# Three small reductions of a hybrid decoder trunk, each computed another way

## The chip, the cores and the metric

The kernel runs on one core of a Trainium2 chip. The metric is the device time of one execution in microseconds. Three executions of the kernel before took 813.9, 815.08 and 815.81 us; the median is 815.08 us.

## The reference

Two decoder layers over 256 tokens of width 1024. A layer normalises the stream, makes one wide projection of it, and feeds three causal mixers side by side: a Mamba-2 state-space branch, sliding-window attention and "forgetting" attention. Each mixer's output is projected back, the three are merged under sigmoid gates, projected once more and added to the residual.

```python
def rms_norm(x, w):
    y = xf * lax.rsqrt(jnp.mean(xf * xf, axis=-1, keepdims=True) + NORM_EPS)
...
for layer in range(DEPTH):
    h = rms_norm(x, norm_w[layer])
    proj = jnp.einsum('bsd,de->bse', h, w_in[layer])          # 1024 -> 12832 columns
    ...
    y_a = mamba2_branch(...)        # dt = softplus(..), a_cum = cumsum(dt * a) in chunks of 128 tokens
    y_b = sliding_window_branch(...)
    y_c = forgetting_attention_branch(...)   # cum = cumsum(log_sigmoid(f)) over all 256 tokens
    branch = jnp.einsum('bsiw,iwd->bsid', ys, w_proj[layer])
    merged = jnp.sum(sigmoid(gates + gate_bias[layer]) * branch, axis=2)
    x = x + jnp.einsum('bsd,de->bse', merged, w_out[layer])
return rms_norm(x, final_norm_w)
```

Three places of it matter here:

- **Row roots.** `rms_norm` of the first layer multiplies each token's row by the reciprocal root of its mean square: 256 numbers.
- **Running sums.** For each layer two running sums over the tokens: 16 heads of the state-space branch (restarting at token 128) and 16 heads of the forgetting attention (running through all 256 tokens).
- **Group sums.** The state-space branch ends in a normalisation of its 1024 channels in 4 groups of 256. For every token and every group, the sum of squares is needed: 4 x 256 numbers a layer.

## The kernel before

Weights are float32 and come from DRAM in pieces of 512 KB through SyncE's queue (L363), into one of six buffers `raw`. ScalarE rounds each piece to a high part `hi` (L293) and VectorE takes the rest as `lo` (L294); both feed TensorE at its fast float32r rate. Activations are kept in the same two parts, and a dense product is three passes: hi x hi, lo x hi, hi x lo. A piece's buffer becomes free, and SyncE can issue a later load into it, when VectorE has made its `lo`.

Products without such parts, the small ones of this document among them, use plain float32, which TensorE does in two passes; each pass is one record of the profile.

The program is a list of operations (`op`, from L1249 on): for each layer the value projections, keys and queries of the window attention, the convolution channels of the state-space branch, then gates and output projections. Small work is launched as a generator (`launch`, L115) that does a part, yields a delay, and is taken up again by `pump` (L150) when the planner's own count of TensorE time, `clock["t"]`, has passed the delay. The delays are constants at the top (`D_CUM`, `D_GN1`, `D_GN2` and so on). So TensorE's order is written out by the planner. The order on the other engines and on SyncE's queue is made by the tile framework's scheduler, except in the first part of the program, whose order is written by hand (L1405 to L1531). `ends_later` holds small pieces of work that are issued after a later operation's eviction (`finish`, L846).

PSUM has two sets of banks: `pmm()` hands out three in turn for the dense products (L78), `pmx()` five for everything else. A bank can be written again only when what was in it has been read by ScalarE or VectorE.

The three places:

- **Row roots** (`normalize`, L1373, first layer only). The first projections are made from the unnormalised stream and scaled as they are read out (`y.rn`, two numbers in each partition: tokens 0 to 127 and 128 to 255). For the keys of the window attention the channels lie in the partitions, so the 256 roots must stand in every partition. ScalarE scales two copies of the identity with the roots (L1377), and TensorE multiplies them by a matrix of ones (L1381), which leaves the roots in a PSUM bank, the same in all partitions. VectorE multiplies the stream by it (L1387), and the result is split into `hi` and `lo` (L1388, by L293 and L294). The keys (`u_bk`, L567) are the first user; the queries (`u_bq`) follow. Each is two halves of 16 matmul records.
- **Running sums** (`decay_logits`, L765). VectorE computes the logits' softplus by a polynomial and leaves the rates in `rates`, as 128 tokens x (2 chunks, 2 kinds, 16 heads). TensorE then makes the running sums with a triangular matrix: L799 with the tokens in the partitions, L801 with the heads in the partitions, one product per chunk, each writing 32 partitions, and L803 adds the first chunk's totals to the second chunk of the forgetting heads. The sums go to DRAM (`cumd`, L810).
- **Group sums** (`group_norms`, L959). `squares` are four tiles, one per group, 128 channels x 256 tokens. With a half of such a tile as weights, a product with two columns of ones gives the sums with the tokens in the partitions: eight products of two columns (L966). VectorE scales them (L968), GpSimd takes the power -1/2 (L969), and VectorE makes a Newton step. The roots are first used in `u_proj_normed` (L980), which stands several operations later.

Of the kernel before, what the change touches and what calls it, by code (L numbers as in the profile page):

```python
# [11 lines left out]
F32 = mybir.dt.float32  # L12
F32R = mybir.dt.float32r
AF = mybir.ActivationFunctionType
ALU = mybir.AluOpType

P = 128
S = 256
# [4 lines left out]
EPS = 1e-6  # L23

D_SOFT, D_SOFT2, D_EVAC, D_SSD, D_SSD2 = 7.0, 3.0, 3.0, 8.0, 4.0
D_K, D_Q, D_QK, D_G0, D_FOX, D_BDMA, D_BIAS, D_BC, D_SSD3 = 6.0, 5.5, 2.0, 8.0, 0.0, 4.0, 2.6, 5.5, 1.0
D_GN1, D_GN2, D_CUM, D_H, D_M = 8.0, 13.5, 17.0, (4.8, 6.4), 5.0
BUDGET = 1.35
T_PP, T_SSD, T_BIAS = 1, 1, 1
D_MEET = 12.0  # L30
# [20 lines left out]
def hybrid_trunk(  # L51
# [5 lines left out]
    nc = tc.nc  # L57
# [5 lines left out]
    dr = ctx.enter_context(tc.tile_pool(name="dr", bufs=1, space=bass.MemoryType.DRAM))  # L63
# [17 lines left out]
    def pmx():  # L81
        return PS("mx", 5)

    act = nc.scalar.activation
    stt = nc.vector.scalar_tensor_tensor
    tt = nc.vector.tensor_tensor
    ts = nc.vector.tensor_scalar
# [15 lines left out]
    def mm(o, a, b, **kw):  # L103
        n = b.free_size()
        if a.dtype == F32R:
            clock["t"] += max(0.094, n / 2350.0)
        else:
            clock["t"] += max(0.2, n / 587.0) * (0.5 if a.free_size() == 64 or a.shape[0] == 32 else 1.0)
        nc.tensor.matmul(o, a, b, **kw)  # L109

    def transpose(o, a, i):
        clock["t"] += 0.109
        nc.tensor.transpose(o, a, i)  # L113
# [76 lines left out]
    ident = T("ident", [P, P])  # L190
    make_identity(nc, ident)
    tri = T("tri", [P, P])
# [11 lines left out]
    ones = onesr.bitcast(F32)  # L204
# [15 lines left out]
    def bc(ap, axis, n):  # L220
        s = list(ap.shape)
        s.insert(axis, n)
        return ap.unsqueeze(axis).to_broadcast(s)
# [66 lines left out]
    def split(hi, lo, src, scale=None, keep=lambda f: f):  # L290

        if scale is None:
            keep(act)(hi, src, AF.Copy)  # L293
            keep(tt)(lo, src, hi.bitcast(F32), op=ALU.subtract)  # L294
        else:
            keep(act)(hi, src, AF.Copy, scale=scale)
            keep(stt)(lo, src, scale, hi.bitcast(F32), op0=ALU.mult, op1=ALU.subtract)
# [130 lines left out]
    for l in range(L):  # L428
        y = Layer()
# [325 lines left out]
    def logits(y, t, i, p):  # L755

        if y.u is None:
            y.u = T("u", [P, 2, 32])
        o, b = y.u[:, t, 16 * i:16 * i + 16], y.hb[:, 16 * i:16 * i + 16]
        tt(o, p, b, op=ALU.add)  # L760
        y.logits += 1
        if y.logits == 4:
            launch(1, decay_logits(y), 0.0)

    def decay_logits(y):  # L765
        u = y.u
# [12 lines left out]
        s2f = s2.rearrange("p t c -> p (t c)")  # L779
        sf = s.rearrange("p t c -> p (t c)")  # L780
        ts(q, s2f, 1.0 / 19.0, None, op0=ALU.mult)
        for m in (17, 15, 13, 11, 9, 7, 5, 3):
            stt(q, q, 1.0 / m, s2f, op0=ALU.add, op1=ALU.mult)
        stt(q, q, 1.0, sf, op0=ALU.add, op1=ALU.mult)
        q3 = q.rearrange("p (t c) -> p t c", t=2)
        y.dt = T("dt", [P, 2, 16])
        rates = T("rates", [P, 2, 2, 16])
        lf = tmp[:, 2, :, 0:16]
        ts(w[:, :, 0:16], u[:, :, 0:16], 0.0, 0.5, op0=ALU.max, op1=ALU.mult)
        tt(y.dt, w[:, :, 0:16], q3[:, :, 0:16], op=ALU.add)  # L790
        ts(y.dt, y.dt, 2.0, None, op0=ALU.mult)
        ts(w[:, :, 16:32], u[:, :, 16:32], 0.0, 0.5, op0=ALU.min, op1=ALU.mult)
        tt(lf, w[:, :, 16:32], q3[:, :, 16:32], op=ALU.subtract)
        ts(rates[:, :, 0, :], lf, -16.0, None, op0=ALU.mult)
        tt(rates[:, :, 1, :], y.dt, bc(y.nega, 1, 2), op=ALU.mult)
        yield D_CUM

        pc = pmx()
        mm(pc[:, P:P + 32], tri, rates[:, :, 1, :], start=True, stop=True)  # L799
        for c in range(2):  # L800
            mm(pc[32 - 32 * c:64 - 32 * c, 0:P], rates[:, c, :, :].rearrange("p w c -> p (w c)"), tri,  # L801
               start=True, stop=(c == 0))
        mm(pc[0:16, 0:P], rates[:, 0, 0, :], ones, start=False, stop=True)  # L803
        y.acum = T("acum", [P, 2, 16])
        act(y.acum, pc[:, P:P + 32].rearrange("p (t c) -> p t c", t=2), AF.Copy)
        cum = T("L1", [64, P])
        act(cum, pc[0:64, 0:P], AF.Copy)
        y.cumd = dr.tile([2, 16, S], F32, name=f"cumd{y.l}", tag=f"cumd{y.l}")
        for c in range(2):
            nc.scalar.dma_start(y.cumd[:, :, c * P:(c + 1) * P].rearrange("w c s -> (w c) s"),  # L810
                                cum[32 - 32 * c:64 - 32 * c, :])


    def u_conv(y, u, c):
# [144 lines left out]
    def group_norms(y, squares):  # L959


        p = pmx()
        for g, q in enumerate(squares):
            for t in range(2):
                c = 4 * g + 2 * t
                mm(p[:, c:c + 2], q[:, t * P:(t + 1) * P], ones[:, 0:2], start=True, stop=True)  # L966
        v, r0 = T("sm", [P, 8]), T("sm", [P, 8])
        ts(v, p[:, 0:16].rearrange("p (g i) -> p g i", i=2)[:, :, 0], 1.0 / 256, 4 * EPS, op0=ALU.mult, op1=ALU.add)  # L968
        gtt(r0, v, mhalf, op=ALU.pow)  # L969

        def newton():
            y.roots = T("rs", [P, 8], bufs=4)
            tt(v, r0, v, op=ALU.mult)
            tt(v, v, r0, op=ALU.mult)
            stt(y.roots, v, -3.0, r0, op0=ALU.add, op1=ALU.mult)

        ends_later.append(newton)
        yield 0.0
# [274 lines left out]
    for y in layers:  # L1253
        l = y.l
        w = w_in[l]
# [8 lines left out]
        def cols(c0, n=256):  # L1264
            return sub([(0, w[:, c0:c0 + n])], n)
# [39 lines left out]
        if l == 0:  # L1305
            v, cv0, cv1 = cols(C_BV), cols(C_CV), cols(C_CV + 256)
            op(v, *(u_bv(y, t, first) for t in range(2)))
            op(None, lambda: layer_consts(y0, nc.gpsimd))
            op(None, lambda: launch(9, normalize(y0), 0.0))
            op(cv0, u_cv(y, 0, 0), u_cv(y, 0, 1))  # L1310
            op(cv1, u_cv(y, 256, 0), u_cv(y, 256, 1))
            gp.pop(0)()
            op(None, lambda: tables(fin["rope"]))
            op(None, lambda: normalized(y0))
        else:
            cv0, v = cols(C_CV, 512), cols(C_BV)
            op(None, lambda: drain(5))
            op(cv0, u_cv(y, 0, 0))
            op(v, u_bv(y, 0))
            op(None, lambda: drain(6))  # L1320
            op(cv0, u_cv(y, 0, 1))
            op(v, u_bv(y, 1))
            gp.pop(0)()
# [48 lines left out]

    def normalize(y):  # L1373

        rb = T("L1", [P, S])
        for t in range(2):
            act(rb[:, t * P:(t + 1) * P], ident, AF.Copy, scale=y.rn[:, t:t + 1])  # L1377
        yield 2.0
        p = pmx()
        for t in range(2):  # L1380
            mm(p[:, t * P:(t + 1) * P], ones, rb[:, t * P:(t + 1) * P], start=True, stop=True)  # L1381
        both_streams(y)
        hTh, hTl = y.normal
        for k in (0, 4):
            for t in range(2):
                xk = xw[:, t, k:k + 4, :]
                tt(xk, xk, bc(p[:, t * P:(t + 1) * P], 1, 4), op=ALU.mult)  # L1387
                split(hTh[:, t, k:k + 4, :], hTl[:, t, k:k + 4, :], xk)  # L1388
        yield 0.0

# [14 lines left out]
    with tc.manual_schedule(engines={ENG.PE, ENG.DVE, ENG.Activation, ENG.Pool}):  # L1405
# [11 lines left out]
        p = pmx()  # L1417
# [93 lines left out]
        for i in range(2):  # L1511
# [57 lines left out]
```

## Time and profile before

| what | value |
|---|---|
| median of three executions | 815.08 us |
| profiled execution, time | 813.07 us |
| its span | 811.4 us |
| TensorE busy | 800.2 us, 99% |
| VectorE busy | 683.8 us, 84% |
| ScalarE busy | 533.4 us, 66% |
| GpSimd busy | 172.7 us, 21% |
| moved by DMA | 170.43 MB, mean 210 GB/s |
| granted TensorE clock | 0.998 |

The span goes from the first instruction to the last; the time of the execution is a little longer. A row of the timeline has the start in us from the span's start, the length in us, the engine (PE is TensorE, DVE VectorE, ACT ScalarE, POOL GpSimd; SPq is SyncE issuing a DMA), the line, the operation, `out<-in`, shapes and a count; in brackets stands how long the engine was idle ahead of it and what ended that. For a matmul, `128*32 128x128` means 128 rows and 32 columns of weights, then the streamed tile. Neighbouring records of the same names are merged into one row, with the shape of the largest. Lines L109 and L113 are the helpers that issue all matmuls and transposes. A DMA row ends in the size of one transfer and the time from issue to landing.

### The profile page before, as it was taken

The page shows a single profiled execution, that of the slowest core. Times are in us where ns is not written, and L with a number is a line of the kernel's source. Part 1 is how long each engine was busy: PE and PEld are TensorE (multiplying, and loading weights), DVE is VectorE, ACT ScalarE, POOL GpSimd, SP SyncE. Part 2 cuts the span into 40 slices and gives each one's busy share as a digit, 9 for nine tenths or more (in the row PEclk, how much of TensorE's full clock was granted, in tenths as well). Part 3 has the DMA queues.
Part 4 walks back from the last instruction along what each step waited for, and adds up shares of the span by engine and source line. Part 5 has one row for each costly group of instructions (what it writes and reads, how often), then busy time and mean ns, then how long its engine had stood idle before and what let it go on. Part 6 is the DMA issues. An engine that isn't in the chain of part 4 may idle for free.

```text
span 811.4 us, 14867 instructions
## 1 busy us (share of the span) xinstructions
PE 800.2 (99%) x5178; PEld 714.2 (88%) x5178; DVE 683.8 (84%) x1412; ACT 533.4 (66%) x1142; POOL 172.7 (21%) x227
## 2 busy tenths in 40 slices
PE   8999999999999999999999999999999999999996
PEld 8998988888888888888998899888888988888896
DVE  6869999978998998776775799999879989869865
ACT  7777767865875785543565678677747677745452
POOL 3167113130321000130001741122313410002000
PEclk9999999999999999999999999999999999999999
DMA  9998888699675565667688987689986645566632
GB/s 311 279 262 183 240 221 203 197 261 252 175 211 163 164 191 180 211 208 246 214 261 259 241 209 220 159 214 257 272 253 175 212 130 160 172 228 218 210 106 77
DMA packets 139418, 170.43 MB, mean 210 GB/s; under 512 B 9976, under 2 KB 107072, under 8 KB 139344
## 3 DMA queue, kind: packets, MB, share of 16 engines
q1 hardware_dynamic: 114960, 140.53, 55.9%
q0 software_dynamic: 12928, 12.68, 9.8%
q10 hardware_dynamic: 11456, 16.28, 7.1%
q8 instruction: 41, 0.67, 0.3%
q14 instruction: 33, 0.27, 0.1%
HBM read 154.71 MB, written 2.16 MB: 193 GB/s over the span
## 4 chain that ended last, share of the span: by engine, by line
PE 96%; DMA 2%; DVE 1%; ACT 1%; issue 0%; SPq 0%; DVEq 0%
PE mm L109 83%; PE mx L109 10%; PE mx L113 3%; DMA raw<-in_w_in_dram 1%; DMA raw<-in_w_proj_dram 1%; DMA hb<-in_sinks_dram 0%; DVE lo L294 0%; ACT L L695 0%; ACT hi L293 0%; SPq L363 0%; SPq L189 0%; DVE L L1431 0%; DVE L L1127 0%; DVE L L1128 0%; ACT L L1435 0%
## 5 line engine op out<-in xcount | busy, mean ns | idle before, releaser
L109 PE MATMUL mm<-L,hi 128*128 128x512 f32 x1056 | 354.6, 387 | 0.3
L294 DVE TENSOR_TENSOR lo<-raw,hi 128x1024 fp32r<-128x1024 f32 (+1 forms) x276 | 313.1, 1153 | 37.8 <-ACT hi L293 36.6
L109 PE MATMUL mm<-hi,L 128*128 128x512 f32 (+2 forms) x1168 | 303.3, 349 | 0.1
L293 ACT ACTIVATE hi<-raw 128x1024 fp32r<-128x1024 f32 (+1 forms) x276 | 265.6, 981 | 51.1 <-PE mm L109 37.1
L109 PE MATMUL mm<-L,lo 128*128 128x256 f32 x1056 | 266.6, 273 | 0.0
L109 PEld LDWEIGHTS mm<-hi,L 128*128 128x128 f32 x1168 | 206.0, 190 | 22.6 <-issue 1.0
L109 PEld LDWEIGHTS mm<-L,hi 128*128 128x128 f32 x1056 | 195.2, 190 | 28.0 <-issue 5.2
L109 PEld LDWEIGHTS mm<-L,lo 128*128 128x128 f32 x1056 | 202.1, 191 | 5.3
L109 PE MATMUL mm<-lo,L 128*128 128x512 f32 (+2 forms) x584 | 201.5, 347 | 0.0
L109 PEld LDWEIGHTS mm<-lo,L 128*128 128x128 f32 x584 | 110.2, 190 | 10.7
L491 POOL DMA_DIRECT2D L<-L x68 | 60.1, 908 | 198.2 <-ACT L L490 153.8
L1057 POOL TENSOR_SCALAR_AFFINE_SELECT bias<-bias 128x128 f32<-128x128 f32 x64 | 40.7, 671 | 69.3 <-DMA bias<-cumd 69.2
L829 DVE SCALAR_TENSOR_TENSOR L<-L,vec,L 128x255 f32<-128x255 f32 (+2 forms) x96 | 46.2, 481 | 2.1 <-ACT L L826 0.3
L489 ACT ACTIVATE L<-mm 128x256 f32<-128x256 f32 x84 | 32.1, 382 | 19.1 <-PE mm L109 15.6
L1091 ACT ACTIVATE L<-L 128x512 f32<-128x512 f32 x24 | 15.1, 631 | 39.9 <-DVE L L1088 31.7
L655 ACT ACTIVATE pp<-pp,nm 128x128 f32<-128x128 f32 x64 | 28.2, 442 | 18.3 <-DVE nm L649 18.3
L613 ACT ACTIVATE pp<-pp,nm 128x128 f32<-128x128 f32 x32 | 12.6, 394 | 25.1 <-DVE nm L618 24.4
L1088 DVE TENSOR_TENSOR L<-mm,L 128x512 f32<-128x512 f32 x22 | 15.1, 686 | 16.4 <-DMA L<-in_gate_bias_dram 8.8
L491 POOL DMA_DIRECT2D qt<-L x16 | 13.8, 860 | 70.9 <-ACT qt L490 69.4
L1124 POOL TENSOR_TENSOR L<-L,L 128x512 f32<-128x512 f32 x8 | 12.8, 1600 | 68.0 <-DVE L L1123 46.2
L490 ACT ACTIVATE L<-mm 128x256 f32<-128x256 f32 x68 | 26.3, 386 | 1.5 <-DMA L<-L 1.5
L835 ACT ACTIVATE L<-L 128x256 f32<-128x256 f32 x32 | 13.4, 418 | 19.0 <-DVE L L829 18.9
(210 smaller groups left out, 913.7 us busy)
## 6 DMA issues: line engine op xcount, KB each, us to landing
raw<-in_w_in_dram SPq DMA_DIRECT2D x191, 512.0 KB, 5.3
raw<-in_w_proj_dram SPq DMA_DIRECT2D x48, 512.0 KB, 5.6
L<-L POOLq DMA_DIRECT2D x72, 128.0 KB, 5.1
raw<-in_w_out_dram SPq DMA_DIRECT2D x16, 512.0 KB, 4.8
bias<-cumd ACTq DMA_DIRECT2D x16, 256.0 KB, 3.7
L<-cumd ACTq DMA_DIRECT2D x8, 512.0 KB, 5.4
L<-in_gate_bias_dram ACTq DMA_DIRECT2D x12, 256.0 KB, 6.2
qt<-L POOLq DMA_DIRECT2D x16, 128.0 KB, 5.5
```

The lines of the kernel that those rows point to most:

```text
L109: nc.tensor.matmul(o, a, b, **kw)
L113: nc.tensor.transpose(o, a, i)
L293: keep(act)(hi, src, AF.Copy)
L294: keep(tt)(lo, src, hi.bitcast(F32), op=ALU.subtract)
L489: act(halves(lo), ordered(p[:, S:2 * S]), AF.Copy)
L490: last = act(halves(out), ordered(p[:, 0:S]), AF.Copy)
L491: nc.gpsimd.dma_start(out, lo, accum_op=ALU.add)
L655: act(pp[:, i, sl], pp[:, i, sl], AF.Exp, scale=-1.0, bias=nm[:, e:e + 1], accum_out=sums[:, e:e + 1])
L829: stt(a[:, s:S], x_[:, 0:S - s], y.vec[:, 16 * j + u:16 * j + u + 1], a[:, s:S], op0=ALU.mult, op1=ALU.add)
L1057: nc.gpsimd.affine_select(out=bias[:, i, dst], in_=bias[:, i, src], compare_op=ALU.is_ge, fill=NEG, base=0, pattern=[[-1, P]], channel_mul ...
L1088: tt(halves(g), p, halves(y.gb), op=ALU.add)
L1091: finish(act(g, g, AF.Tanh, scale=0.5))
```

## The change

- **Group sums.** The squares become the streamed operand: 32 columns of ones are the weights, and each of the four groups writes its own 32 partitions of one bank, in 256 columns. ScalarE copies the bank to SBUF; after a delay `D_GN2`, now 3.0 and not used before, two transposes bring the tokens back into the partitions, and VectorE picks one of every 32 columns.
- **Running sums.** The rates are written into a zeroed tile of 128 columns per kind of use (`all_` and `past`); GpSimd does the zeroing. One product of 128 weight columns with the triangle, and one with the ones for the carried totals, add up in one bank. The product of L799 is unchanged. The two chunks now lie in the other order in the partitions, and the transfer to DRAM follows.
- **Row roots.** Instead of the scaled identities and the product, SyncE's queue writes the roots to DRAM (`row`, 256 numbers of 4 bytes) and reads them back to all partitions (`rb`). VectorE multiplies by `rb` in SBUF. The planner's delay between the two parts is 6.0 instead of 2.0.

```diff
-D_GN1, D_GN2, D_CUM, D_H, D_M = 8.0, 13.5, 17.0, (4.8, 6.4), 5.0
+D_GN1, D_GN2, D_CUM, D_H, D_M = 8.0, 3.0, 17.0, (4.8, 6.4), 5.0
...
-        rates = T("rates", [P, 2, 2, 16])
+        wide = T("L1", [P, 2, P])
+        nc.gpsimd.memset(wide, 0.0)
+        all_, past = wide[:, 0, :], wide[:, 1, :]
+        rates = all_[:, 0:64].rearrange("p (t w c) -> p t w c", t=2, w=2)
...
         tt(rates[:, :, 1, :], y.dt, bc(y.nega, 1, 2), op=ALU.mult)
+        ts(past[:, 32:48], lf[:, 0, :], -16.0, None, op0=ALU.mult)
         yield D_CUM
 
         pc = pmx()
+        mm(pc[:, 0:P], all_, tri, start=True, stop=False)
+        mm(pc[:, 0:P], past, ones, start=False, stop=True)
         mm(pc[:, P:P + 32], tri, rates[:, :, 1, :], start=True, stop=True)
-        for c in range(2):
-            mm(pc[32 - 32 * c:64 - 32 * c, 0:P], rates[:, c, :, :].rearrange("p w c -> p (w c)"), tri,
-               start=True, stop=(c == 0))
-        mm(pc[0:16, 0:P], rates[:, 0, 0, :], ones, start=False, stop=True)
...
-                                cum[32 - 32 * c:64 - 32 * c, :])
+                                cum[32 * c:32 + 32 * c, :])
...
         for g, q in enumerate(squares):
-            for t in range(2):
-                c = 4 * g + 2 * t
-                mm(p[:, c:c + 2], q[:, t * P:(t + 1) * P], ones[:, 0:2], start=True, stop=True)
+            mm(p[32 * g:32 * g + 32, 0:S], ones[:, 0:32], q, start=True, stop=True)
+        r = T("L1", [P, S])
+        act(r, p[:, 0:S], AF.Copy)
+        yield D_GN2
+        p = pmx()
+        for t in range(2):
+            transpose(p[:, t * P:(t + 1) * P], r[:, t * P:(t + 1) * P], ident)
...
-        rb = T("L1", [P, S])
-        for t in range(2):
-            act(rb[:, t * P:(t + 1) * P], ident, AF.Copy, scale=y.rn[:, t:t + 1])
-        yield 2.0
-        p = pmx()
-        for t in range(2):
-            mm(p[:, t * P:(t + 1) * P], ones, rb[:, t * P:(t + 1) * P], start=True, stop=True)
+        row = dr.tile([2, P], F32, name="row", tag="row")
+        nc.sync.dma_start(row.rearrange("t p -> p t"), y.rn[:, 0:2])
+        rb = T("L1", [P, S])
+        nc.sync.dma_start(rb, row.rearrange("t p -> (t p)").partition_broadcast(P))
+        yield 6.0
...
-                tt(xk, xk, bc(p[:, t * P:(t + 1) * P], 1, 4), op=ALU.mult)
+                tt(xk, xk, bc(rb[:, t * P:(t + 1) * P], 1, 4), op=ALU.mult)
```

In the program that results, TensorE's order is the same outside these blocks. In SyncE's queue `row` stands behind the load that was issued at 17.02 us before, and `rb` two loads further on. On VectorE the splits of the two weight pieces that stood behind the products with the roots now stand ahead of them.

More of the change, by code (lines that the diff above doesn't have):

```diff
@@ L963, in group_norms @@
         for g, q in enumerate(squares):
-            for t in range(2):
-                c = 4 * g + 2 * t
-                mm(p[:, c:c + 2], q[:, t * P:(t + 1) * P], ones[:, 0:2], start=True, stop=True)
+            mm(p[32 * g:32 * g + 32, 0:S], ones[:, 0:32], q, start=True, stop=True)
[5 more added lines that the diff above has]
+            transpose(p[:, t * P:(t + 1) * P], r[:, t * P:(t + 1) * P], ident)
         v, r0 = T("sm", [P, 8]), T("sm", [P, 8])
-        ts(v, p[:, 0:16].rearrange("p (g i) -> p g i", i=2)[:, :, 0], 1.0 / 256, 4 * EPS, op0=ALU.mult, op1=ALU.add)
+        ts(v.rearrange("p (g t) -> p t g", t=2), p[:, 0:S].rearrange("p (t g i) -> p t g i", t=2, i=32)[:, :, :, 0],
+           1.0 / 256, 4 * EPS, op0=ALU.mult, op1=ALU.add)
         gtt(r0, v, mhalf, op=ALU.pow)
```

## The prediction

> **What bounds the kernel now.** I read the page first: shares of the engines, then the chain that ended last.
>
> ```profile
> span 811.4 us, 14867 instructions
> PE 800.2 (99%) x5178; PEld 714.2 (88%) x5178; DVE 683.8 (84%) x1412; ACT 533.4 (66%) x1142; POOL 172.7 (21%) x227
> PE 96%; DMA 2%; DVE 1%; ACT 1%; issue 0%; SPq 0%; DVEq 0%
> ```
>
> TensorE is busy 99% of the span and is 96% of the chain. So two things count: how much TensorE time the edits add or remove, and whether TensorE will now have to wait somewhere. The profiled run took 813.07 us (span 811.4), 2.0 below the median of 815.08; the sum is made against 813.07 and carried over to the median.
>
> For TensorE I read the timeline and take the distance from one start to the next, since the durations shown overlap.
>
> **Group sums, before.** The timeline of PE at the first layer's group sums:
>
> ```profile
> 313.51 0.59 PE L109 MATMUL mm<-hi,L 128*128 128x512 f32 x2
> ...
> 314.16 1.84 PE L109 MATMUL mx<-ones,L 128*128 128x2 f32 x16
> 315.86 0.68 PE L109 MATMUL mm<-hi,L 128*128 128x512 f32 x2
> ```
>
> Eight float32 products are 16 records, two passes each. From 314.16 to 315.86 is 1.70 us, and the pair behind them takes 0.68 instead of 0.59, so 1.79 us a layer: 0.11 per pass, though each streams only two columns. Below, a pass of 128 or fewer columns at 128 weight columns is taken at 0.11.
>
> **Running sums, before.**
>
> ```profile
> 118.08 0.38 PE L109 MATMUL mm<-L,hi 128*128 128x512 f32 x1
> 118.30 0.30 PE L109 MATMUL mx<-rates,tri 128*128 128x32 f32 x2
> 118.53 0.41 PE L109 MATMUL mx<-tri,rates 128*32 128x128 f32 x4
> ...
> 119.09 0.48 PE L109 MATMUL mm<-L,hi 128*128 128x512 f32 x1
> 119.41 0.38 PE L109 MATMUL mm<-L,lo 128*128 128x256 f32 x2
> ```
>
> A product `hi` is followed by the next start 0.22 later (118.08 to 118.30). Without the block, the `lo` of 119.41 would have started at 118.30 + 0.22 = 118.52; the block costs 0.89 us. Some 0.2 of it is the way back to full width: 0.32 from 119.09 to 119.41 instead of 0.22, and as much in the gap before.
>
> After: three products over the whole array, six passes of 0.11 = 0.66, no change of width. Saved 0.23 a layer, **0.46** in both.
>
> **Row roots, before.**
>
> ```profile
> 20.41 0.39 PE L109 MATMUL mm<-hi,L 128*128 128x256 f32 x2
> 20.64 0.28 PE L109 MATMUL mm<-lo,L 128*128 128x256 f32 x1
> 20.75 0.61 PE L109 MATMUL mx<-L,ones 128*128 128x128 f32 x4
> 21.11 0.47 PE L109 MATMUL mm<-hi,L 128*128 128x256 f32 x2
> 21.42 0.28 PE L109 MATMUL mm<-lo,L 128*128 128x256 f32 x1
> ```
>
> A pair of `hi` normally takes 0.23 to the `lo` (20.41 to 20.64); so 21.42 - 0.23 - 20.75 = **0.44** us that TensorE no longer spends.
>
> **Group sums, after.** Four products of 32 weight columns, 256 streamed columns, each to its own 32 partitions of one bank. No row shows four column tiles; the nearest are the two-wide column tiles (128*64) of the attention values, the four-wide row tiles (32*128) of its scores, and float32 over the full array:
>
> ```profile
> 110.99 0.38 PE L109 MATMUL mm<-L,hi 128*128 128x512 f32 x1
> 111.30 1.52 PE L109 MATMUL mx<-L,bias 128*64 128x256 f32 x16
> 112.65 1.47 PE L109 MATMUL mm<-L,bias 128*64 128x256 f32 x16
> 114.05 1.59 PE L109 MATMUL mx<-L,qt 32*128 32x128 f32 x32
> 115.58 0.48 PE L109 MATMUL mm<-L,hi 128*128 128x512 f32 x1
> 115.89 0.38 PE L109 MATMUL mm<-L,lo 128*128 128x256 f32 x2
> ...
> 194.52 0.82 PE L109 MATMUL mx<-L 128*128 128x256 f32 x4
> 195.09 0.68 PE L109 MATMUL mm<-hi,L 128*128 128x512 f32 x2
> ```
>
> The full array does two passes of 256 and two of 128 columns from 194.52 to 195.09, with 0.09 more in the pair after: 0.66, so 0.22 a pass of 256. The 16 passes from 112.65 to 114.05 are half 256, half 128 columns: one at a time 8 x 0.22 + 8 x 0.11 = 2.64, they took 1.40, so two run at once. The 32 passes from 114.05 to 115.58 would be 5.3 one at a time and took 1.53: with row tiles four run at once. Going in costs 0.09 (110.99 to 111.30 is 0.31, not 0.22) and about 0.05 in the first pass, coming out 0.2 (115.58 to 115.89 is 0.31; the gap before it as much over). With four at once: 2 x 0.21 + 0.35 = 0.77; two at once 1.2; one at a time 2.1. I take four, as the tiles share neither columns nor output partitions and both kinds of tile in the trace overlap fully. The two transposes are one pass each, 0.22, so 0.99 a layer: saved 0.80, **1.60** in both (ends: 0.76 saved with two at once, 1.08 lost one at a time).
>
> [...]
>
> **What is hidden there.** The copy of the sums to SBUF and the wait for it lie under one whole gate unit of 24 passes at 0.22, 5.2 us, which the TensorE order has between the sums and the transposes; two further units follow before the roots are first read. Without that cover TensorE would wait for the copy, some 0.4, once a layer. The memset of the padded rates goes to GpSimd, 21% busy, where it stands ahead of the first convolution transfer after the logits; VectorE writes into the tile only at the end of its polynomial:
>
> ```profile
> 116.17 0.17 DVE L794 TENSOR_SCALAR rates<-L 128x32 f32<-128x32 f32 x1
> ```
>
> VectorE's extra copy of 16 columns is another 0.17, of the 2.1 between 116.17 and TensorE's 118.30. Apart from the blocks named, TensorE's order is the same, block for block; ScalarE loses the two scaled copies of the identity.
>
> **Row roots, after: the transfers.** Both go through SyncE's queue, which brings the weights. In the changed order `row` stands behind the load issued at 17.02, then two loads follow (the 19.03 and 20.16 ones of before), then `rb`, which waits for `row` and holds up all later loads. Rows: the end of the roots, then, by window, landing times of the loads issued at 17.02, 21.97 and 23.11, and what the engines moved from 22.5 to 24:
>
> ```profile
> 17.69 0.16 DVE L238 TENSOR_TENSOR rs<-sm,sm 128x2 f32<-128x2 f32 x1
> 17.02 0.37 SPq L363 DMA_DIRECT2D raw<-in_w_in_dram  x1
> 21.97 0.37 SPq L363 DMA_DIRECT2D raw<-in_w_in_dram  x1
> raw<-in_w_in_dram SPq DMA_DIRECT2D x1, 512.0 KB, 5.5
> raw<-in_w_in_dram SPq DMA_DIRECT2D x1, 512.0 KB, 7.8
> raw<-in_w_in_dram SPq DMA_DIRECT2D x1, 512.0 KB, 8.1
> DMA packets 569, 0.52 MB, mean 349 GB/s; under 512 B 43, under 2 KB 569, under 8 KB 569
> ```
>
> `row` can go at 17.9 but its packets queue behind a load that lands at 22.5; estimate 22.9. `rb` is issued at about 23.1, behind two loads of 512 KB. The load after those landed at 29.8 and takes 1.5 us at 349 GB/s, so they are in by 28.3; 128 KB more is 0.4: `rb` lands at X = 28.7. The loads it holds up leave 1.2 to 1.5 us late, and VectorE splits the first of them only at 34.43: hidden.
>
> **What waits for X.** In the changed VectorE order the four products with `rb` stand ahead of all that follows:
>
> ```profile
> 23.00 1.88 DVE L1387 TENSOR_TENSOR L<-L,mx 128x512 f32<-128x512 f32 x3
> 27.80 4.75 DVE L294 TENSOR_TENSOR lo<-raw,hi 128x1024 fp32r<-128x1024 f32 x6
> 32.48 0.74 DVE L1090 SCALAR_TENSOR_TENSOR L<-mm,rs,L 128x512 f32<-128x512 f32 x1
> 34.43 3.70 DVE L294 TENSOR_TENSOR lo<-raw,hi 128x512 fp32r<-128x512 f32 x6 [1.22 <-ACT hi L293]
> 42.35 0.38 ACT L490 ACTIVATE L<-mm 128x256 f32<-128x256 f32 x1
> 37.05 0.46 PE L109 MATMUL mm<-L,hi 128*128 128x512 f32 x1
> 37.30 26.20 PE mm L109 x160
> ```
>
> Before, VectorE ran without a gap from 23.00 to the gate's read at 32.48: eight operations of the normalisation and, from 27.80, two full weight splits and four half ones, 9.48 us in all. The two full ones, half of 4.7, now come ahead of X. So the read is at X + 7.1 instead of 32.48. From it hangs a chain on ScalarE: tanh, splits, the second gate's tanh, the rope tables, and the first key half's evictions, which end at 42.35 + 0.38 = 42.73. They free one of three banks for the first query group's second half. The key halves start at 37.05; ten halves of 16 records take 26.20, so 2.62 each, and the fourth starts at 44.91. Slack 2.18, less the 0.44 that TensorE is now earlier: 1.74. TensorE stalls for X + 7.1 - 32.48 - 1.74 = X - 27.1. At X = 28.7 that is **1.6 us**, and nothing later gives it back, since TensorE is the bound to the end.
>
> **Sum.** -0.44 - 0.46 - 1.60 + 1.6 = -0.9: 812.2 profiled, 814.2 by the median. A measurement of this kernel can tell about 0.2%, 1.63 us, from no change; so I forecast within that.
>
> **Rivals.**
> Hidden transfers: if X is 27.1 or less, nothing stalls and the whole 2.5 stays: 812.6, faster. For it: transfers of 16 KB out of the rates landed in 2.1 (row below), and two of those from 17.9 end at 22.1. Against: those met an idle queue.
>
> ```profile
> cumd<-L ACTq DMA_DIRECT2D x4, 16.0 KB, 2.1
> ```
>
> [...]
>
> Late transfers (slower): `rb` waits as long as its neighbours in the queue, 8.1 us from 23.1, so X = 31.2, or `row`, with its 256 packets of 4 bytes (no row shows such a write), lands two microseconds later than taken. Place: the same wait at the first query group. From X = 29.6 on the change loses; at 31.2 it loses 1.6, at 32 it loses 2.4: 817.5.
>
> Column tiles that don't overlap: two at once keeps 0.76 of the 1.60, and with the stall the sum is -0.1: 815.0. One at a time gives -0.44 - 0.46 + 1.08 + 1.6 = +1.8: 816.9.
>
> **How the numbers follow.** Forecast 0.46, hidden 0.22, late 0.20, no overlap 0.12 (0.08 two at once, 0.04 one). Of the forecast, X between 28 and 30 gives -1.6 to +0.4, so nearly all of it is within the bound; I give 0.06 to faster and 0.03 to slower. Faster 0.22 + 0.06 = 0.28; slower 0.20 + 0.03 + 0.04 = 0.27; same 0.45. The range runs from hidden transfers less a little for the spread of the medians, 811.9, to the late case, 817.5; the forecast's own is 813.4 to 815.5.
>
> **What would show it.** Sums: four starts a few nanoseconds apart, twice, 0.2 apart, and the block at about 0.8. Running sums: six passes 0.11 apart with no long step after. Transfers: `row` landing near 23, `rb` near 28.7, VectorE idle from about 25 until then on the DMA, and TensorE idle once near 44 on ScalarE. Wrong if VectorE starts its products with `rb` before 27 or after 30, if TensorE idles elsewhere, or if the column tiles start 0.2 apart.

## The result, and the profile after

The changed kernel takes 818.35 us (median of six runs, 816.26 to 819.25), the kernel before 813.64 (six runs, 812.91 to 815.81). The ratio is 1.0057, with a 95% interval of 1.0045 to 1.0070: slower by 4.7 us where 0.9 less had been forecast, and outside the range. The profiled run took 816.26, the lowest of its six. Its page opens so (shares of the engines, and of the chain that ended last):

```profile
span 814.6 us, 14835 instructions
PE 800.6 (98%) x5158; PEld 712.3 (87%) x5158; DVE 684.5 (84%) x1414; ACT 533.3 (65%) x1142; POOL 186.8 (23%) x229
PE 94%; DMA 2%; DVE 2%; ACT 1%; issue 0%; SPq 0%; DVEq 0%
```

TensorE is busy 98% instead of 99%, and its share of the chain fell from 96% to 94%; that of VectorE rose from 1% to 2%, that of the DMA stays at a rounded 2%. The chain itself, in order of time (start, length, what), says where:

```profile
17.23 9.88 DMA row<-rs
...
27.13 4.50 DMA L<-row
...
31.65 2.50 DVE L L1392 x4
...
37.21 5.42 PE mm L109 x31
...
44.54 0.67 DVE L L1097
...
45.35 6.79 PE mm L109 x30
```

`row`, 1 KB, takes 9.88 us from its issue at 17.23 and lands at 27.11 (predicted 22.9). `rb` is issued at once behind it, needs another 4.50, and VectorE starts at X = 31.65 (predicted 28.7). VectorE's timeline, its wait and the two reads of the gate (L1097):

```profile
31.65 2.50 DVE L1392 TENSOR_TENSOR L<-L,L 128x512 f32<-128x512 f32 x4 [5.83 <-DMA L<-row]
...
38.88 0.74 DVE L1097 SCALAR_TENSOR_TENSOR L<-mm,rs,L 128x512 f32<-128x512 f32 x1
...
44.46 0.74 DVE L1097 SCALAR_TENSOR_TENSOR L<-mm,rs,L 128x512 f32<-128x512 f32 x1
```

The first read stands at X + 7.23, as predicted (7.1). The second frees the bank for which TensorE has waited since 42.6. The two longest of TensorE's waits that the kernel before does not have, a window of all engines (the last three figures are TensorE's granted clock, the DMA share and GB/s), the eviction on ScalarE that frees the next bank, and the pair of records whose second opens the fourth half:

```profile
PE mm L109 <- DVE L L1097: 2.7, 1, 2.7
PE mm L109 <- DVE lo L294: 0.6, 1, 0.6
```

```profile
45.40:48.80 3.40, 3.40 (x11) 2.95 (x12) 0.72 (x2) 3.31 (x9) 0.00 (x0) 0.51 0.90 282
```

```profile
48.76 0.38 ACT L490 ACTIVATE L<-mm 128x256 f32<-128x256 f32 x1
```

```profile
49.47 0.60 PE L109 MATMUL mm<-L,hi 128*128 128x512 f32 x2
```

Behind the wait TensorE runs 3.4 us at half the clock (0.51), which no step of the prediction had. The blocks of the sums are as short as predicted. Both in the changed kernel, TensorE's timeline:

```profile
122.77 0.38 PE L109 MATMUL mm<-L,hi 128*128 128x512 f32 x1
122.99 0.38 PE L109 MATMUL mx<-tri,L 128*128 128x128 f32 x2
123.21 0.39 PE L109 MATMUL mx<-ones,L 128*128 128x128 f32 x2
123.43 0.31 PE L109 MATMUL mx<-L,tri 128*128 128x32 f32 x2
123.58 0.46 PE L109 MATMUL mm<-L,hi 128*128 128x512 f32 x1
123.87 0.39 PE L109 MATMUL mm<-L,lo 128*128 128x256 f32 x2
...
318.76 0.38 PE L109 MATMUL mm<-lo,L 128*128 128x512 f32 x1
319.07 0.64 PE L109 MATMUL mx<-L,ones 128*32 128x256 f32 x8
319.64 0.70 PE L109 MATMUL mm<-hi,L 128*128 128x512 f32 x2
320.18 0.38 PE L109 MATMUL mm<-lo,L 128*128 128x512 f32 x1
```

Running sums: without the block the `lo` of 123.87 would stand 0.22 behind 122.99, so it costs 0.66, as predicted. Group sums: 0.57 from 319.07 to 319.64, 0.09 more in the gap ahead (0.31 instead of 0.22), 0.11 more in the pair behind (0.54 instead of 0.43): 0.77, as predicted, so four column tiles do run at once. Laid record by record beside the kernel before, TensorE gains 0.23 at each running sum and 0.80 at each group sum (1.02 less 0.22 for the two transposes).

The 0.23 of a running sum does not last. Six us behind the block stand transposes of `pp`, the weights of the window attention, which VectorE has to scale first (L642). The kernel before, VectorE's row and TensorE's two; then the changed kernel:

```profile
123.46 0.69 DVE L642 TENSOR_TENSOR pp<-pp,rsum 128x512 f32<-128x512 f32 x1
124.22 0.38 PE L109 MATMUL mm<-L,hi 128*128 128x512 f32 x1
124.44 0.60 PE L113 MATMUL mx<-ident,pp 128*128 128x128 f32 x4
```

```profile
128.25 0.69 DVE L642 TENSOR_TENSOR pp<-pp,rsum 128x512 f32<-128x512 f32 x1
128.68 0.38 PE L109 MATMUL mm<-L,hi 128*128 128x512 f32 x1
129.09 0.63 PE L113 MATMUL mx<-ident,pp 128*128 128x128 f32 x4
```

From the product to the transposes it was the usual 0.22; now it is 0.41: counted from the start of the running sums, TensorE comes 0.23 earlier and VectorE, with its extra copy, has its result 0.10 later. With 0.03 in the transposes themselves, 0.22 of the 0.23 is given back, and as much in the second layer.

### The profile page after: what moved, and what is told of

Its sections match the earlier page's. It is cut to its first block, busy times and chain, and to the rows that moved or that the text cites. A ratio compares the mean times of both kernels' runs of the same rounds, so it can differ in the third digit from the quotient of the medians.

```text
span 814.6 us, 14835 instructions
## 1 busy us (share of the span) xinstructions
PE 800.6 (98%) x5158; PEld 712.3 (87%) x5158; DVE 684.5 (84%) x1414; ACT 533.3 (65%) x1142; POOL 186.8 (23%) x229
## 4 chain that ended last, share of the span: by engine, by line
PE 94%; DMA 2%; DVE 2%; ACT 1%; issue 0%; SPq 0%; DVEq 0%
PE mm L109 81%; PE mx L109 9%; PE mx L113 4%; DMA row<-rs 1%; DVE lo L294 1%; DMA L<-row 1%; DMA L<-in_x_dram 0%; DVE L L1392 0%; DVE L L294 0%; ACT hi L1449 0%; DVE L L1095 0%; DVE lo L1455 0%; ACT L L1440 0%; ACT L L244 0%; ACT L L695 0%
## 5 line engine op out<-in xcount | busy, mean ns | idle before, releaser
L1064 POOL TENSOR_SCALAR_AFFINE_SELECT bias<-bias 128x128 f32<-128x128 f32 x64 | 53.5, 871 | 66.0 <-DMA bias<-cumd 65.2
L489 ACT ACTIVATE L<-mm 128x256 f32<-128x256 f32 x84 | 32.1, 382 | 18.1 <-PE mm L109 13.7
L655 ACT ACTIVATE pp<-pp,nm 128x128 f32<-128x128 f32 x64 | 28.2, 442 | 18.2 <-DVE nm L649 18.2
L976 POOL TENSOR_TENSOR sm<-sm,mhalf 128x8 f32<-128x8 f32 x2 | 5.2, 2592 | 105.9 <-DVE sm L974 105.9
L490 ACT ACTIVATE L<-mm 128x256 f32<-128x256 f32 x68 | 26.4, 388 | 1.7 <-DMA L<-L 1.7
L1095 DVE TENSOR_TENSOR L<-mm,L 128x512 f32<-128x512 f32 x22 | 15.1, 687 | 11.4 <-PE mm L109 9.1
```

The costliest lines, as they stand in the source:

```text
L489: act(halves(lo), ordered(p[:, S:2 * S]), AF.Copy)
L490: last = act(halves(out), ordered(p[:, 0:S]), AF.Copy)
L655: act(pp[:, i, sl], pp[:, i, sl], AF.Exp, scale=-1.0, bias=nm[:, e:e + 1], accum_out=sums[:, e:e + 1])
L1064: nc.gpsimd.affine_select(out=bias[:, i, dst], in_=bias[:, i, src], compare_op=ALU.is_ge, fill=NEG, base=0, pattern=[[-1, P]], channel_mul ...
L1095: tt(halves(g), p, halves(y.gb), op=ALU.add)
```

## The experiments

The kernel before was measured anew beside each group of runs (medians 812.7 to 813.45); ratios are to it.

### Which part loses: the sums alone, and the transfers alone

`e1_no_transfer` is the changed kernel with the old `normalize`:

```diff
-        row = dr.tile([2, P], F32, name="row", tag="row")
-        nc.sync.dma_start(row.rearrange("t p -> p t"), y.rn[:, 0:2])
...
+        for t in range(2):
+            act(rb[:, t * P:(t + 1) * P], ident, AF.Copy, scale=y.rn[:, t:t + 1])
```

> The changed kernel with the row roots as they were (two scaled identities and a product by ones); group sums and running sums stay changed. Theory A, the transfers carry the whole loss: the time is that of before less the savings read in the two profiles (0.36 for the running sums, 1.70 for the group sums), about 2.1 us under before (ratio 0.9975), and TensorE does not wait at the first query group's second half more than before. Rival B, a part of the loss lies in the new sums (memset of the padded rates, copies on ScalarE, later stages): between before and 2 us above it (ratio 1.000 to 1.0025).

Measured: 811.05 us (11 runs), ratio 0.9980 (0.9971 to 0.9988), about 2.0 under before. TensorE shows neither of the two waits above. Theory A by the time, but it comes to the expected 2.1 partly by luck: in this profile, too, each running sum gives its gain back (0.23 won, 0.21 lost), and TensorE waits twice for VectorE's read of a gate (L1095, 0.42 at 151 and 0.35 at 548), which the kernel before does not; a wait for VectorE at the start of the second layer (L1128, 1.17 at 364 in the kernel before) is gone instead. That last wait differs from profile to profile, with the old sums too (0.27 in `e2`, 1.9 in `g1`), so how the 2.0 divides is not shown.

`e2_transfer_alone` is the kernel before with the new `normalize` alone (the same diff the other way round).

> The kernel before with the row roots by transfers alone; the sums stay old. Theory A, the transfers carry the whole loss: 5 to 7 us above before (ratio 1.006 to 1.009), with the write of the roots landing near 27, their return near 31.6, the wait of TensorE at the first query group near 42 to 45, and the granted clock near 0.5 for some 3 us behind it. Rival B, part of the loss is in the sums: 3 us above before or less (ratio 1.004 or less).

Measured: 821.09 us, ratio 1.0106 (1.0090 to 1.0123): 8.1 us slower, a little more than expected. The chain of waits holds the same two links, later still:

```profile
16.78 10.53 DMA row<-rs
...
27.32 5.04 DMA L<-row
...
32.39 2.50 DVE L L1385 x4
```

So the changed kernel without its transfers is some 2 us quicker, and the transfers lose more than all of it.

### Which transfer, and is it its place in the queue

`e4_no_row` leaves out the write and spreads 256 numbers of x instead:

```diff
-        nc.sync.dma_start(row.rearrange("t p -> p t"), y.rn[:, 0:2])
...
-        nc.sync.dma_start(rb, row.rearrange("t p -> (t p)").partition_broadcast(P))
+        nc.sync.dma_start(rb, x2[0:1, 0:S].to_broadcast([P, S]))
```

> The changed kernel without the write of the roots: the spread transfer reads 256 numbers of x from DRAM instead, so the rows are scaled by wrong numbers and the output is not the reference's; all else stays. Theory S, the write is what comes late: the spread is issued at about 17.3, lands behind two loads at 23 to 25, VectorE does not wait for it beyond 27, and the time is some 2.1 to 2.5 under before (ratio 0.997). Rival R, the spread itself (128 packets of 1 KB behind the loads of its queue) is late enough: it lands after 28, and the kernel is no faster than before (ratio 1.000 or more).

Measured: 811.03 us, ratio 0.9976 (0.9966 to 0.9986). Nothing holds the spread up now, so it is issued at 15.34, ahead of the roots, and VectorE goes on at 22.33:

```profile
22.33 0.69 DVE L1390 TENSOR_TENSOR L<-L,L 128x512 f32<-128x512 f32 x1 [2.11 <-DMA L<-in_x_dram]
```

The spread alone costs nothing here (7.0 us from issue to landing, all under other work); it is the write that is late. Since the spread no longer waits for the roots, the run does not say what a quick write would leave.

`e3_act_queue` issues both transfers from ScalarE:

```diff
-        nc.sync.dma_start(row.rearrange("t p -> p t"), y.rn[:, 0:2])
+        nc.scalar.dma_start(row.rearrange("t p -> p t"), y.rn[:, 0:2])
...
```

> The changed kernel with both transfers of the roots issued by ScalarE instead of SyncE, so that they stand behind no weight load in their queue. Theory Q, the place behind the loads makes them late: the write lands 2 to 3 us after its issue (near 20.5), the return near 23 to 25, VectorE does not wait beyond 27, and the time is some 2.1 to 2.5 under before (ratio 0.997). Theory S, the write of 256 packets of 4 bytes is slow by itself: it lands 6 us or more after its issue, the return comes after 27, and the kernel is between 0.5 under and 4 us above before (ratio 0.9995 to 1.005).

Measured: 818.70 us, ratio 1.0073 (1.0058 to 1.0087). With no load ahead of it in its queue the write still takes 9.55 us: Theory S, and somewhat above its end of 1.005. ScalarE's timeline also shows what a waiting issue does to an engine that has work: it stands 6.48 us, and the weight splits behind it are late.

```profile
18.21 0.41 ACTq L1383 DMA_DIRECT2D row<-rs  x1
...
27.78 0.34 ACTq L1385 DMA_DIRECT2D L<-row  x1
28.17 0.47 ACT L1026 ACTIVATE L<-mm,rs 128x256 f32<-128x256 f32 x1 [6.48 <-DMA row<-rs]
```

That changes where TensorE stalls: its longest wait is 2.49 us, up to 28.69, for this eviction (L1026), with half clock behind it. So the landing is a clean test of the queue, the time is not.

### What makes the write slow

`f1_eight_bytes` keeps the row in the order token, chunk, so that each partition sends its two numbers as one packet:

```diff
-        row = dr.tile([2, P], F32, name="row", tag="row")
-        nc.sync.dma_start(row.rearrange("t p -> p t"), y.rn[:, 0:2])
+        row = dr.tile([P, 2], F32, name="row", tag="row")
+        nc.sync.dma_start(row, y.rn[:, 0:2])
...
-                tt(xk, xk, bc(rb[:, t * P:(t + 1) * P], 1, 4), op=ALU.mult)
+                tt(xk, xk, bc(rb.rearrange("q (p t) -> q t p", t=2)[:, t, :], 1, 4), op=ALU.mult)
```

> The changed kernel with the row of roots kept in the order token, then chunk: the same 1 KB is written as 128 packets of 8 bytes instead of 256 of 4, at the same place of the same queue, and VectorE reads the spread roots with a stride of two. Theory S, the write's time goes by the count of its packets: its last part lands some 3 to 5 us earlier (22 to 24 instead of 27.1), the spread near 28 to 29, the wait of TensorE shrinks below 1 us without a stretch of half clock, and the time is 814 to 815.5 (ratio 1.000 to 1.003). Rival T, any write that leaves 128 partitions at this moment takes as long, whatever its packets: landing near 27 and 817.5 to 819.5 as the changed kernel (ratio 1.0055 to 1.008).

Measured: 815.19 us, ratio 1.0024 (1.0014 to 1.0034). The write lands at 23.68, in 6.25 us, and X is 29.72; the landing and the time are as Theory S said. The spread is not back at 28 to 29, as it also said, but at 29.70, and TensorE's wait is not below 1 us but 2.4 here and 1.5 later (0.98 at 47.9 and 0.57 at 79.4). VectorE's four products, which read the roots with a stride of two here, take 3.15 us instead of 2.50; those 0.65 us are not the write's:

```profile
23.70 0.34 SPq L1385 DMA_DIRECT2D L<-row  x1
```

```profile
29.72 3.15 DVE L1392 TENSOR_TENSOR L<-L,L 128x512 f32<-128x512 f32 x4 [4.77 <-DMA L<-row]
```

`f2_two_packets` turns the roots into two rows on TensorE first:

```diff
-        nc.sync.dma_start(row.rearrange("t p -> p t"), y.rn[:, 0:2])
+        p = pmx()
+        transpose(p[0:2, 0:P], y.rn[:, 0:2], ident)
+        rt = T("rt", [2, P])
+        act(rt, p[0:2, 0:P], AF.Copy)
+        nc.sync.dma_start(row, rt)
```

> The changed kernel with the roots transposed by TensorE and copied by ScalarE first, so that the same 1 KB is written as 2 packets of 512 bytes. Its write is issued later, since the transpose stands behind some products and the write behind two more loads. Theory S: the write lands 2 to 4 us after its own issue, the spread near 27 to 29, and the time is 812 to 814.5 (ratio 0.9985 to 1.002). Rival T, the moment and not the packets make it slow: 7 us or more from issue to landing, and the time is that of the changed kernel or above (ratio 1.005 or more).

Measured: 812.86 us, ratio 0.9996 (0.9987 to 1.0005). The write takes 5.14 us, but from 19.93, and its spread is behind yet another load: X is 30.35. The time is in the range of Theory S; the 5.14 is a us over its 2 to 4, and X a us behind its 29. TensorE waits 1.8 us for ScalarE's evictions (L490), about what this kernel has over the sums alone. They are 0.39 at 44.7 and 1.40 at 77.3. The first is far less than an X of 30.35 costs by the prediction's rule (3.25), since the scheduler put VectorE's read of the gate elsewhere: ahead of the last splits, at X + 4.82, where the changed kernel has it at X + 7.23:

```profile
35.17 0.74 DVE L1097 SCALAR_TENSOR_TENSOR L<-mm,rs,L 128x512 f32<-128x512 f32 x1
```

The first key half's evictions end at 44.66, X + 14.3, instead of X + 17.5. So this time is that of a quicker write and of another order on VectorE together.

Eight bytes and half the packets went together in `f1`; the next four look at packets, size and place. They are all the kernel before with a write that nobody waits for, the roots still going through the product by ones. `e5_row_alone` adds the changed kernel's write:

```diff
+        row = dr.tile([2, P], F32, name="row", tag="row")
+        nc.sync.dma_start(row.rearrange("t p -> p t"), y.rn[:, 0:2])
```

> The kernel before with the 4-byte write of the roots added and nothing that waits for it; the roots still go through the product by ones. Theory W, only the wait for the roots costs time: the write lands about 10 us after its issue and the weight loads behind it 2 to 3 us later than in the kernel before, but VectorE and TensorE have them in time: ratio 0.9985 to 1.0015. Theory N, the loads that it delays cost time by themselves: ratio 1.002 or more, with TensorE or VectorE waiting for a weight split.

Measured: ratio 1.0019 (1.0010 to 1.0028), between the two theories. The write takes 10.07 us, and the load behind it lands at 30.36 (that of before at 25.56); TensorE waits once for a split, 0.4. A write alone costs little more than what a measurement can tell; the stall needs the wait.

`g2_half_row` writes one chunk (128 packets of 4 bytes, side by side); `g1_apart` writes all 256, each 256 bytes from the next; `h1_apart64` the same at 64 bytes (16 in place of the 64 below). The edits of the first two, against `e5_row_alone`:

```diff
-        nc.sync.dma_start(row.rearrange("t p -> p t"), y.rn[:, 0:2])
+        nc.sync.dma_start(row[0:1, :].rearrange("t p -> p t"), y.rn[:, 0:1])
```

```diff
-        row = dr.tile([2, P], F32, name="row", tag="row")
-        nc.sync.dma_start(row.rearrange("t p -> p t"), y.rn[:, 0:2])
+        row = dr.tile([2, P, 64], F32, name="row", tag="row")
+        nc.sync.dma_start(row.rearrange("t p c -> p t c")[:, :, 0:1],
+                          y.rn[:, 0:2].rearrange("p (t o) -> p t o", o=1))
```

> As the kernel before with the write of the roots alone, but of the first chunk only: 128 packets of 4 bytes side by side. Theory N, the number of packets sets the time: about 6 us from issue to landing, as for the 128 packets of 8 bytes (6.25). Theory B, it is the size of 4 bytes: about 10 us still.

> As the kernel before with the write of the roots alone, but the 256 numbers of 4 bytes go to places 256 bytes apart in DRAM. Theory N, the number of packets sets the time: the write lands about 10 us after its issue and the DMA engines again move under 150 GB/s between 22 and 28. Theory L, packets to neighbouring places in DRAM hold each other up: it lands 4 to 6 us after its issue, and the engines keep 200 GB/s or more.

> As the kernel before with the write of the roots alone, its 256 numbers of 4 bytes placed 64 bytes apart in DRAM instead of 256. Theory L64, packets hold each other up only inside one stretch of 64 bytes: it lands about 5.2 us after its issue, as at 256 bytes apart. Theory L512, the stretch is longer (two numbers or more of 4 bytes share it at 64 apart): 6 to 8 us.

Measured, with the other writes; landed is the last update of the transfer's semaphore in the trace:

| run | the write | issued | landed | us |
|---|---|---|---|---|
| changed kernel | 256 x 4 B, side by side | 17.23 | 27.11 | 9.88 |
| `e2`, `e3`, `e5` | the same | 16.78, 18.21, 17.66 | 27.31, 27.76, 27.73 | 10.53, 9.55, 10.07 |
| `g2_half_row` | 128 x 4 B, side by side | 17.93 | 27.47 | 9.54 |
| `f1_eight_bytes` | 128 x 8 B, side by side | 17.43 | 23.68 | 6.25 |
| `h1_apart64` | 256 x 4 B, 64 B apart | 17.44 | 23.07 | 5.63 |
| `g1_apart` | 256 x 4 B, 256 B apart | 17.75 | 22.91 | 5.16 |
| `f2_two_packets` | 2 x 512 B | 19.93 | 25.07 | 5.14 |

Half the packets of 4 bytes are no quicker (Theory N falls, B holds), and all 256 of them are nearly as quick as two large ones once they lie 64 bytes apart, and as quick at 256 (Theory L, L64). So neither their number nor their size alone makes them slow: it takes small packets that go to the same stretch of DRAM. `f1` limits this: its 128 packets of 8 bytes lie side by side too and land in 6.25, against 9.54 for as many of 4 bytes. Whether there the size counts, or how many share a stretch (64 bytes hold 8 of them, or 16 of 4 bytes), was not taken apart. Theory S, which counts packets, had the landing of `f1` right by luck. The DMA engines show it for everything that runs then. Windows of two us, the last figure in GB/s: the kernel before, the changed kernel, `g2`, `g1`.

```profile
22.00:24.00 2.00, 2.00 (x21) 2.00 (x20) 2.00 (x3) 2.00 (x3) 0.00 (x0) 1.00 0.93 303
24.00:26.00 2.00, 2.00 (x21) 2.00 (x20) 2.00 (x5) 1.91 (x4) 0.00 (x0) 1.00 1.09 148
26.00:28.00 2.00, 2.00 (x14) 1.84 (x13) 2.00 (x5) 1.89 (x4) 1.48 (x3) 1.00 0.96 320
```

```profile
22.00:24.00 2.00, 2.00 (x20) 2.00 (x20) 1.39 (x2) 1.81 (x3) 0.00 (x0) 1.00 0.99 137
24.00:26.00 2.00, 2.00 (x19) 1.97 (x18) 1.73 (x2) 0.92 (x2) 0.00 (x0) 1.00 0.54 87
26.00:28.00 2.00, 2.00 (x11) 1.74 (x10) 0.00 (x0) 0.00 (x0) 0.05 (x1) 1.00 0.63 101
```

```profile
22.00:24.00 2.00, 2.00 (x20) 2.00 (x19) 2.00 (x3) 2.00 (x4) 0.00 (x0) 1.00 2.06 161
24.00:26.00 2.00, 2.00 (x20) 2.00 (x20) 2.00 (x4) 1.95 (x4) 0.00 (x0) 1.00 0.44 25
26.00:28.00 2.00, 2.00 (x14) 1.84 (x14) 2.00 (x5) 0.63 (x1) 0.00 (x0) 1.00 0.77 63
```

```profile
22.00:24.00 2.00, 2.00 (x21) 2.00 (x20) 2.00 (x3) 2.00 (x3) 0.00 (x0) 1.00 1.05 311
24.00:26.00 2.00, 2.00 (x21) 2.00 (x20) 2.00 (x5) 1.80 (x5) 0.31 (x1) 1.00 1.00 123
26.00:28.00 2.00, 2.00 (x14) 1.81 (x13) 2.00 (x4) 2.00 (x5) 0.60 (x2) 1.00 1.02 345
```

From 22 to 28, 303, 148 and 320 become 137, 87 and 101, and the weights are late with it, those of another queue too (in `e3` SyncE's load issued at 18.95 lands at 30.38; the one of 19.03 in the kernel before at 25.56); with the packets apart, the figures of before are back (the dip to 123 lies in a window where before has one too). `g1`'s time is 1.0022 (1.0012 to 1.0032), `h1`'s 1.0008 (0.9997 to 1.0020), `g2`'s 1.0012 (1.0002 to 1.0022). So a lone write costs up to 0.2%, with quick writes as with slow ones (`h1`'s interval includes none). In the profiles of `g1` and `g2` TensorE runs as before, record by record, but for one wait for VectorE at the start of the second layer (L1128), which is 0.45 us longer than in the profile of before; that is not all of the time, and why the wait changes is open.

### Does the half clock cost its own

`f4_fill` gives TensorE 24 products to do where it waits (a transpose of the identity, which nobody reads), `g3_fill_two` the same at both places where it was seen to wait:

```diff
+            p = pmx()
+            for _ in range(24):
+                nc.tensor.transpose(p[:, 0:P], ident, ident)
+            u0(w)
```

> The changed kernel with 24 idle transposes of the identity (2.6 us by 0.11 each) put on TensorE ahead of the first query half, where it waits 2.7 us for VectorE's gate read; nothing reads them. Theory C, the half clock behind that wait comes from TensorE's idleness and costs about 1.7 us of its own: the query half starts as late as in the changed kernel, the granted clock is 1.00 behind it, and the time is 1 to 2 us under that of the changed kernel (ratio to before 1.003 to 1.0065). Rival D, the half clock has another cause: 0.5 is granted all the same, and the time is that of the changed kernel (ratio 1.0055 to 1.008).

> The changed kernel with 24 idle transposes ahead of the first key half and 24 more ahead of the first query half, the two places where TensorE was seen to wait for VectorE; nothing reads them. Theory C, the half clock follows TensorE's idleness and costs about 1.7 us of its own: the granted clock stays 1.00 from 36 to 52, and the time is 1 to 2 us under that of the changed kernel (ratio to before 1.003 to 1.0065, the lower half likelier). Rival D, what ends the stall is VectorE's and ScalarE's chain behind the late roots, whatever TensorE's clock: the time is that of the changed kernel (1.0055 to 1.008).

Measured: `f4_fill` 818.69 us, ratio 1.0067 (1.0054 to 1.0080). In its profile `row` took 11.02 and X was 33.85, so that TensorE waited 1.2 and 1.3 at the first key half, where there is no fill, and ran at half clock there; its fill covered the other place, and no half clock followed. `g3_fill_two` 818.60, ratio 1.0080 (1.0067 to 1.0094): the fill took up both waits, the clock stays whole, and nothing is won. X is 32.88 here. TensorE's waits on ScalarE, its granted clock and what stops it next (of the two waits in the first row the other, 1.19, is at 82.5):

```profile
PE mm L109 <- ACT L L490: 1.9, 2, 1.2
```

```profile
46.00:48.00 2.00, 2.00 (x17) 1.92 (x16) 1.03 (x2) 1.69 (x5) 0.00 (x0) 1.00 0.95 275
```

```profile
44.30 2.79 PE L572 MATMUL mx<-ident 128*128 128x128 f32 x24
...
50.41 0.48 PE L109 MATMUL mm<-L,hi 128*128 128x512 f32 x1 [0.70 <-ACT L L490]
```

Theory C falls, Rival D holds: TensorE, quick again, meets ScalarE's eviction (L490) half a head further on, which is the wait that the prediction had named. The end of the stall is set by the chain from X: the first evictions end at X + 17.5 in the changed kernel, `e2`, `f4` and `g3` alike, with half clock and without. So the half clock mostly fills time in which TensorE would have waited.

## Why the prediction was wrong

The "late transfers" rival is what happened, past its end of 817.5 by the median.

**Product of the row roots** (-0.44): right; no such block is left.

**Running sums** (-0.46): the block is right (0.66, so 0.23 saved in each), but the saving was not kept, and this is a second step that failed. The prediction set VectorE's extra copy against the 2.1 us ahead of the product and did not look at what VectorE does next: its scaling of `pp` was just in time before, and TensorE now waits for it. 0.22 of each 0.23 is given back, so the term was worth about nothing.

**Group sums** (-1.60): right (0.77, four at once, and 0.22 for the transposes; 0.80 saved in each). The row of the score passes from which four at once was argued shows 128 columns; half of its 32 passes stream 256, as the prediction's 5.3 has it. The memset, the copy of the sums and the wait for it were hidden as said.

So the three are worth 2.1, not 2.5. The sums alone are 2.06 in the prediction and 2.0 in `e1` by the medians, the latter with the luck told there.

**Where `row` lands: the step that failed, and the largest error.** The prediction let it queue behind a load and put its landing at 22.9. Packets of 4 bytes that lie 64 or 256 bytes apart did land at 23.07 and 22.91; side by side, as the kernel has them, at 27.11 and later. The rival had named those packets with two us for them; they cost over four, and slow the loads around them (137, 87 and 101 GB/s from 22 to 28, for 303, 148 and 320 before). No trace here shows how a write is done; the times show a price for packets of 4 bytes only where they are neighbours, since 5.16 us for 256 of them apart is no more than the 5.14 of two of 512.

The landing does not explain all of the loss. In `f1` it was 23.68, near the forecast, and the kernel still lost some 2 us, where the prediction's sum has +0.1 for its X of 29.72. The 0.65 of its slower products and the 0.46 of the running sums are part of the difference; the rest lies in waits further on that no step had.

**From there to X**: `rb` took 4.50 us from its issue, against 5.6 predicted. X came out at 31.65 in this profile, and at 32.39, 33.42, 33.85 and 32.88 in the profiles of `e2`, `e3`, `f4` and `g3`, so the one shown has the earliest X of five. The median, 2.1 over the profiled run, would fit the others; X was not seen in the runs without a profile.

**The hidden-transfers rival**: its 2.1 us a transfer was not seen; the quickest write took 5.14 (`f2`), and no spread less than 4.4 (4.50 in the changed kernel; in `g3` issued at 28.42, with VectorE at 32.88).

**The price of X**: the rule X - 27.1 was right in its mechanism, for the order that VectorE has in the changed kernel. The bank comes free at 49.14 = X + 17.5 (predicted X + 17.35), and by the rule the stall at 31.65 is 4.55. The fourth half starts at 49.69 instead of 44.56 (45.00 in the kernel before, which the prediction had at 44.91, less 0.44), so it was 5.1: the half clock carried TensorE 0.55 past the eviction. With the 2.1 of the savings that makes +3.0, of the 3.2 between the two spans. Later waits change by some tenths both ways; that nothing gives the stall back is not quite so, as the wait at 364 (L1128) is 0.4 shorter than before.

**The place**: TensorE was to idle once near 44 on ScalarE. With X three us later it idled at 42.6, on VectorE's second read of the gate, one half sooner; the slack there was not worked out. From the rows it is an estimate of X = 28.2: the third half starts at 45.35 = X + 13.7, and without a stall it would start at 41.94 (42.38 in the kernel before, less 0.44). So even at the forecast X of 28.7 the wait would have begun there. The place predicted is seen as well, but only where that other wait is shorter or filled: 0.98 in `f1`, 0.79 in `e3`, 0.70 in `g3`, 0.39 in `f2`.

## What to carry to other kernels

The column that became a row in DRAM was here not 1 KB but at least one small packet per partition (256 of 4 bytes, or 128 of 8 in `f1`), and the packets of 4 bytes held each other up, and the loads beside them, when they lay side by side (9.54 to 11.02 us from issue to landing; 64 bytes apart was enough for 5.63): turn the data round on the chip and write large packets (5.14 for two of 512 bytes), or place them apart, or don't go through DRAM at all (the product by ones cost 0.44 us of TensorE, the transfers 7.3, changed kernel less `e1`, to 8.1, `e2`). Where an engine's slack is a chain that ends in several places, work out each place, since the stall sits at the first that is late. Time saved on the busiest engine lasts only as far as the next thing it needs from another engine: look past the block for it (0.22 of 0.23 was gone six us later). And split a change: here two of its three parts were together worth 2 us, which the third hid.

## What the runs showed of the hardware that was not expected

- Writes of 4 bytes side by side in DRAM: 9.5 to 11.0 us for 128 or 256 of them; 64 bytes apart 5.63. Meanwhile, from 22 to 28, all of the core's DMA moved 25 to 161 GB/s (`g2`, changed kernel) instead of 148 to 320 (before). Why their place in DRAM does so was not seen.
- TensorE's granted clock fell to half (0.50) for about 3.4 us behind single waits of 2.74 (changed kernel), 2.73 (`e2`) and 2.49 us (`e3`) and behind two of 1.23 and 1.26 close together (`f4`), and not behind 2.43 (`f1`). What decides between 2.43 and 2.49, and what sets the length of 3.4, was not shown.
